# Hybrid decoder block: second buffers for the block rows and columns, masks and products with CB on VectorE, other waits for the delta heads

## The chip, the cores and the metric

The kernel runs on one core of one Trainium2 chip. The metric is the device time of one execution in microseconds (us), as the median of several runs.

## What is computed

One decoder layer for 256 tokens of width 2048 in float32: a SwiGLU (5632 wide) with half weight, a mixer of 8 delta heads (128 wide) and 16 state-space heads (64 wide) between one input and one output projection, a second SwiGLU, a gated per-layer embedding, and a final norm. Cut to what the change touches:

```python
def gated_delta_rule_chunked(q, k, v, g, beta):
    gc = jnp.cumsum(g, axis=-1)
    decay = jnp.exp(jnp.where(causal, gc[..., :, None] - gc[..., None, :], -jnp.inf))
    lower = jnp.where(strict, jnp.einsum('bnhik,bnhjk->bnhij', kb, k) * decay, 0.0)
    t_inv = lax.linalg.triangular_solve(eye + lower, eye, left_side=True, lower=True)
    ...
def ssd_chunked(x, dt, a_neg, bm, cm):
    seg = jnp.exp(jnp.where(causal, acs[..., :, None] - acs[..., None, :], -jnp.inf))
    cb = jnp.einsum('bnlgd,bnsgd->bngls', cc, bc)
    y_diag = jnp.einsum('bngrls,bnsgrp->bnlgrp', cb[:, :, :, None] * seg, xc)
    ...
h = h + 0.5 * swiglu(rmsnorm(h, ffn1_norm), ...)
proj = rmsnorm(h, mix_norm) @ w_in
o_gdn = gdn_mixer(...)   # delta heads
o_ssm = ssd_mixer(...)   # state-space heads
h = h + jnp.concatenate([o_gdn, o_ssm], axis=-1) @ w_out
```

## The kernel before

**Main work.** All activations lie transposed (features on the partitions). Every large weight is loaded in float32 by SyncE's queue (L110), and each piece of 128x1024 is split into a rounded part `hi` by ScalarE (L118) and the remainder `lo` by VectorE (L119); TensorE then multiplies `hi` and `lo` with the split activations. In the mixer `single` (L135) does this: a tile of 128 columns of `w_in` is two pieces, a piece is 24 matmuls (three each for eight blocks, L145 to L147). `project` makes two tiles, `conv_silu` lets the short convolution (L557) and SiLU follow, `silu_gate` the gate.

**Side work.** After every piece `tick` (L174) steps each generator in the list `side` once, up to its next `yield`. The generators are the scalars of the heads (`scalars`), the decay matrices (`early_decays`, `late_decay`), a pair of delta heads (`gdn_pair`, four times) and four state-space heads (`ssd_quad`, four times). A `yield` thus says how many pieces of main work are emitted between two steps. The order in which the instructions of an engine stand in its queue is made at build time by a planner (`schedule_with_timeline_sim=True`): emission gives the rank, and the planner's own model of times decides what is ready. Each engine then works its queue off in order.

**Decay.** A row of summed gates is spread over the partitions by DMA (`spread`, L447, tile `hT`, which is free in this stage). `decay` adds the causal mask to it, 128x512 at a time, on GpSimd (L453): one instruction for a pair, two for a quad, so 12 in all. ScalarE exponentiates (L457). `ssd_quad` multiplies the quad's decay with `CB` on GpSimd (L820), two instructions of 128x512 for each quad, 8 in all, before the matmuls of L832 read them.

**A pair of delta heads.** `kk` products (L596) and decay give `LA`. Its 32x32 blocks on the diagonal are written to DRAM by four DMAs of GpSimd's queue (L630, `blkl`) and come back with the block rows on the partitions (`Lb`, L632, SyncE's queue). VectorE then solves 31 columns one after the other (L663 and L665, `tb` and `Z`, 62 short instructions, `STEP = 3` columns for each tick), the result goes to DRAM (`blky`, L666) and back in four DMAs (`Y`, L671), and after `WAIT = 4` ticks VectorE transposes it (L674, `oT`). The blocks of 32 are put together to 64 and 128 by matmuls (`ip`, `ix`, `iy`, L685), then follow the products with the values (`two`, L714), the norm of the heads, four ticks, and the transposes back (`ot`, L758). `Lb` and `Z` have one buffer each (4 KB and 512 B of a partition), so a pair's block rows and columns wait for the pair before it; `qs` (1 KB) and `o` (2 KB) have one buffer of their own, `S` has one, `xv` two.

**Order of the mixer.** Pair 0, keys, pair 1, keys, pair 2, quad 0, pair 3, quads 1 to 3, then gates. Pair 3 has 40 ticks between its start and the point where the main work drains it, and its generator has 38 `yield`s once its decay is ready.

Of the kernel before, what the change touches and what calls it, by code (L numbers as in the profile page):

```python
# [9 lines left out]
F32 = mybir.dt.float32  # L10
F32R = mybir.dt.float32r
AF = mybir.ActivationFunctionType
ALU = mybir.AluOpType
PSUM = bass.MemoryType.PSUM

P = 128
# [27 lines left out]
BS = 32  # L44
CG = 4
# [4 lines left out]
WAIT = 4  # L50
STEP = 3
# [17 lines left out]
def tile_hybrid_block(ctx, tc, xT, pT, con, par, wgu1, wd1, wnar, win, wout, wgu2, wd2, wproj, wple, outT):  # L69
    nc = tc.nc  # L70
    act, dve, pool, pe = nc.scalar, nc.vector, nc.gpsimd, nc.tensor
# [17 lines left out]
    ident, upper, cmask = (cont[:, i * P:(i + 1) * P] for i in range(3))  # L89
# [3 lines left out]
    def pv(name):  # L93
        o, c = POFF[name]
        return part[:, o:o + c]

    def over(ap, n):
        return ap.unsqueeze(1).to_broadcast([ap.shape[0], n, ap.shape[-1]])
# [5 lines left out]
    def mx_bank(name):  # L104
        return psx.tile([P, 512], F32, tag="mx", name=name)
# [256 lines left out]
    with ExitStack() as mix:  # L362
# [76 lines left out]
        def quad_dec(i):  # L439
            k = (8, 12, 0, 4)[i]  # L440
            return hT[:, k:k + 4, :].rearrange("p k (n i) -> p (k n) i", i=P).rearrange("p (c n) i -> p c n i", c=2)
# [7 lines left out]
        def decay(d, h0, n):  # L449

            flat = d.rearrange("p c n i -> p (c n) i")
            for m in range(0, 2 * n, 4):
                pool.tensor_tensor(out=flat[:, m:m + 4], in0=flat[:, m:m + 4], in1=over(cmask, 4), op=ALU.add)  # L453
            yield
            yield
            for m in range(2 * n):
                act.activation(flat[:, m, :], flat[:, m, :], AF.Exp,  # L457
                               bias=ngc[:, m // n, h0 + m % n:h0 + m % n + 1])
                if m % 2:
                    yield  # L460

        def quad_decay(i):


            d = quad_dec(i)
            ers[i] = m2.tile([P, 2, P], F32, tag="er", name="er")
            for hh in range(2):
                s = slice(64 * hh, 64 * hh + 64)
                act.activation(ers[i][s], d[s, 1].rearrange("p (j h) l -> p h j l", h=2)[:, hh], AF.Exp)
            yield from decay(d, 8 + 4 * i, 4)  # L470
            ready.add(("quad", i))
# [3 lines left out]
        def early_decays():  # L475
            for i in range(4):
                spread(pair_dec(i), rows[:, 2 * i:2 * i + 2, :])
                if i:
                    yield
            for i in range(2):  # L480
                yield from decay(pair_dec(i), 2 * i, 2)
                ready.add(("pair", i))
            for i in range(2):
                spread(quad_dec(i), rows[:, 8 + 4 * i:12 + 4 * i, :])
                yield
            for i in range(2, 4):
                yield from decay(pair_dec(i), 2 * i, 2)
                ready.add(("pair", i))
            for i in range(2):
                yield from quad_decay(i)  # L490
# [85 lines left out]
        def gdn_pair(i, KQ, V):  # L576
# [16 lines left out]
            for c in range(2):  # L593
# [5 lines left out]
                for hh in range(2):  # L599
                    m = 2 * c + hh  # L600
# [6 lines left out]
                              in1=beta[:, :, h0:h0 + 2], op=ALU.mult)  # L607
            for m, (c, hh) in enumerate(mats):
                dve.scalar_tensor_tensor(
                    out=LA[:, m, :, :], in0=kk[c][:, hh * T:(hh + 1) * T].rearrange("p (a i) -> p a i", a=2),  # L610
# [17 lines left out]
            parts = [slice(q * BS, (q + 1) * BS) for q in range(P // BS)]  # L628
            for q, p in enumerate(parts):
                nc.gpsimd.dma_start(bl.rearrange("(m b) j i -> b j m i", m=4)[q], LT[p, :, p])  # L630
            Lb = g2.tile([P, BS, BS], F32, tag="Lb", name="Lb", bufs=1)
            nc.sync.dma_start(Lb.rearrange("p j i -> p (j i)"),  # L632
                              bl.rearrange("q j i -> q (j i)").unsqueeze(1).to_broadcast([P // NG, NG, BS * BS]))
            Z = g2.tile([P, CG, BS], F32, tag="Z", name="Z", bufs=1)
            tb = g2.tile([P, CG * BS], F32, tag="tb", name="tb", bufs=1)

            Y = g2.tile([P, 4, P], F32, tag="Y", name="Y")
# [6 lines left out]
            xv = g2.tile([P, 4, P], F32, tag="xv", name="xv")  # L644
# [9 lines left out]
            for _ in range(4):  # L654
                yield
            dve.tensor_copy(Z, unit)

            for j in range(BS - 1):
                if j % STEP == 0:
                    yield  # L660
                n = BS - 1 - j
                t = tb[:, :CG * n].rearrange("p (c n) -> p c n", n=n)
                dve.tensor_tensor(out=t, in0=over(Lb[:, j, j + 1:], CG),  # L663
                                   in1=Z[:, :, j:j + 1].to_broadcast([P, CG, n]), op=ALU.mult)
                dve.tensor_tensor(out=Z[:, :, j + 1:], in0=Z[:, :, j + 1:], in1=t, op=ALU.subtract)  # L665
            nc.gpsimd.dma_start(by.rearrange("q c i -> (q c i)").rearrange("(p f) -> p f", p=P),  # L666
                              Z.rearrange("p c i -> p (c i)"))

            X = oT[:, h0:h0 + 2, :].rearrange("p n (m i) -> p (n m) i", i=P)
            for q, p in enumerate(parts):  # L670
                nc.gpsimd.dma_start(Y[p, :, p], by.rearrange("(m b) c i -> b c m i", m=4)[q])  # L671
            for _ in range(WAIT):
                yield
            dve.transpose(X, Y)  # L674

# [16 lines left out]
            S = g2.tile([P, 2, P], F32, tag="S", name="S", bufs=1)  # L692
# [21 lines left out]
                    pe.matmul(ps[:, hh * P:(hh + 1) * P], lhs[hh], rhs[:, hh, :], start=True, stop=True)  # L714
                return ps[:, 0:T].rearrange("p (h v) -> p h v", h=2)

            qs = g2.tile([P, 2, P], F32, tag="qs", name="qs", bufs=1)
            o = g2.tile([P, 4, P], F32, tag="o", name="o", bufs=1)
            y0, y1 = xv[:, 0:2, :], xv[:, 2:4, :]
            ps = two([Y[:, hh, :] for hh in range(2)], y0, "y0")  # L720
            act.copy(y0, ps)
# [9 lines left out]
            for hh in range(2):  # L731
                dve.scalar_tensor_tensor(out=y1[:, hh, :], in0=pk[:, hh, :], scalar=negc[:, h0 + hh:h0 + hh + 1],
                                         in1=y1[:, hh, :], op0=ALU.mult, op1=ALU.add)
# [17 lines left out]
            pool.tensor_tensor(out=ro, in0=ro, in1=rq, op=ALU.mult)  # L751
            for m in range(4):
                act.mul(o[:, m, :], o[:, m, :], ro[:, m:m + 1])
            for _ in range(4):
                yield
            ps = mx_bank("ot")
            for m, (c, hh) in enumerate(mats):
# [4 lines left out]
        g2 = gdn_pool.enter_context(tc.tile_pool(name="g2", bufs=2))  # L762
# [20 lines left out]
        CB = mp.tile([P, 4, P], F32, name="CB")  # L783
# [15 lines left out]
        def ssd_quad(i, XS):  # L799

            g = i // 2
            h0 = 4 * i
            while ("quad", i) not in ready:
                yield
            d, er = quad_dec(i), ers[i]
            ds = [d[:, c] for c in range(2)]
            yield
            ps = mx_bank("xt")
            for c in range(2):
                for j in range(2):  # L810
                    pe.transpose(ps[:, (2 * c + j) * P:(2 * c + j + 1) * P], XS[:, j, c * P:(c + 1) * P], ident)
            xd = m2.tile([P, 2, 4, 64], F32, tag="xd", name="xd", bufs=1)
            for c in range(2):
                dve.tensor_tensor(out=xd[:, c], in0=ps[:, c * T:(c + 1) * T].rearrange("p (h v) -> p h v", h=4),
                                  in1=dt[:, c, h0:h0 + 4].unsqueeze(2).to_broadcast([P, 4, 64]), op=ALU.mult)
            xe = m2.tile([P, 4, 64], F32, tag="xe", name="xe", bufs=1)
            dve.tensor_tensor(out=xe, in0=xd[:, 0],
                              in1=dte[:, 8 + h0:12 + h0].unsqueeze(2).to_broadcast([P, 4, 64]), op=ALU.mult)
            for c in range(2):
                pool.tensor_tensor(out=ds[c], in0=ds[c], in1=over(CB[:, 2 * c + g, :], 4), op=ALU.mult)  # L820
            yield
            yield
            ps = mx_bank("ss0")
            pe.matmul(ps[:, 0:T], Bt[:, g, :], xe.rearrange("p h v -> p (h v)"), start=True, stop=True)
            St = m2.tile([P, 2, P], F32, tag="St", name="St", bufs=1)
            act.copy(St, ps[:, 0:T].rearrange("p (j v) -> p j v", j=2))
            yield
            py = mx_bank("py")
            for j in range(2):
                for hh in range(2):  # L830
                    for c in range(2):
                        pe.matmul(py[hh * 64:(hh + 1) * 64, j * T + c * P:j * T + (c + 1) * P],  # L832
                                  xd[:, c, 2 * j + hh, :], ds[c][:, 2 * j + hh, :], start=True, stop=True)
            ps = mx_bank("yo")
            for j in range(2):
                pe.matmul(ps[:, j * P:(j + 1) * P], St[:, j, :], BC[:, 1, g, P:T], start=True, stop=True)
            dve.tensor_tensor(out=er, in0=ps[:, 0:T].rearrange("p (j l) -> p j l", j=2), in1=er, op=ALU.mult)
            for j in range(2):
                t = 2 * i + j
                dve.scalar_tensor_tensor(out=yT[:, t, :], in0=XS[:, j, :], scalar=pv("sd")[:, t:t + 1],  # L840
                                         in1=py[:, j * T:(j + 1) * T], op0=ALU.mult, op1=ALU.add)
            dve.tensor_tensor(out=yT[:, 2 * i:2 * i + 2, P:T], in0=yT[:, 2 * i:2 * i + 2, P:T], in1=er, op=ALU.add)
# [53 lines left out]
        op = mix.enter_context(tc.tile_pool(name="op", bufs=1))  # L896
# [183 lines left out]
```

## Time and profile before

| | |
|---|---|
| median of 3 runs | 2077.48 us (2076.0 to 2078.01) |
| the profiled execution | 2078.17 us |
| its span, first to last instruction | 2076.3 us |
| TensorE busy | 2050.2 us, 99% of the span |
| VectorE, ScalarE, GpSimd busy | 1364.6, 1036.3, 174.5 us |
| mean granted clock of TensorE | 0.995 |

Times in the rows are microseconds from the first instruction, durations are microseconds unless marked ns. PE is TensorE, DVE VectorE, ACT ScalarE, POOL GpSimd, SP SyncE; SPq is the queue of DMAs that SyncE issues. Line numbers are those of the kernel before. The mixer lies between about 770 and 1207 us.

### The profile page before, as it was taken

How to read it: one execution, taken by the hardware profiler on the slowest of the kernel's cores; microseconds unless marked ns; L12 is line 12 of the kernel's file. 1: busy time of each engine (PE TensorE's matmuls, PEld its weight loads, DVE VectorE, ACT ScalarE, POOL GpSimd, SP SyncE). 2: the span in 40 equal slices, each digit the busy share in tenths (PEclk: the TensorE clock that was granted, in tenths of full speed). 3: DMA queues.
4: the chain of work that ended last, by engine and by line, in shares of the span. 5: the costliest groups of instructions: out<-in, count | busy, mean ns of one | idle time of the engine just before them, and what ended most of it. 6: DMA issues, size and time to landing. Idle time of an engine off the chain costs nothing.

```text
span 2076.3 us, 31518 instructions
## 1 busy us (share of the span) xinstructions
PE 2050.2 (99%) x12882; PEld 1833.7 (88%) x12882; DVE 1364.6 (66%) x2060; ACT 1036.3 (50%) x1542; POOL 174.5 (8%) x207
## 2 busy tenths in 40 slices
PE   9999999999999999999999999999999999999997
PEld 7888888888888889989999998888888888888886
DVE  7565555555656669999887666556555565556675
ACT  6444444444444556645545456444444444445554
POOL 2000000000000013313321111000000000000011
PEclk9999999999999999999999999999999999999998
DMA  7555555655555666544544555555556555545652
GB/s 263 191 185 183 173 175 192 210 183 185 189 182 178 198 223 213 180 165 163 176 166 168 186 182 186 196 185 183 168 182 217 184 183 185 190 162 189 207 183 102
DMA packets 64369, 384.58 MB, mean 185 GB/s; under 512 B 7616, under 2 KB 9168, under 8 KB 31072
## 3 DMA queue, kind: packets, MB, share of 16 engines
q1 hardware_dynamic: 61456, 376.75, 52.6%
q0 software_dynamic: 2480, 5.29, 0.8%
q8 instruction: 101, 1.65, 0.3%
q10 hardware_dynamic: 288, 0.52, 0.1%
q14 instruction: 44, 0.36, 0.0%
HBM read 377.78 MB, written 4.75 MB: 184 GB/s over the span
## 4 chain that ended last, share of the span: by engine, by line
PE 91%; DVE 3%; DMA 2%; issue 2%; POOL 1%; ACT 1%; POOLq 0%; DVEq 0%; SPq 0%; ACTq 0%
PE mm L130 50%; PE mm L128 24%; PE mm L146 4%; PE mm L147 4%; PE mm L145 4%; PE mm L132 1%; DMA hT<-rows 1%; DVE lo L119 1%; DVE u L557 1%; PE pj L130 0%; PE ip L685 0%; DMA blky<-Z 0%; DMA blkl<-LA 0%; PE iy L685 0%; POOL hT L820 0%
## 5 line engine op out<-in xcount | busy, mean ns | idle before, releaser
L119 DVE TENSOR_TENSOR lo<-raw,hi 128x1024 fp32r<-128x1024 f32 (+1 forms) x774 | 859.0, 1117 | 481.2 <-ACT hi L118 480.6
L130 PE MATMUL mm<-xs,hi 128*128 128x512 f32 x3088 | 1078.4, 397 | 1.1 <-DVE xs L190 1.0
L118 ACT CAST hi<-raw 128x1024 fp32r<-128x1024 f32 (+1 forms) x774 | 745.3, 964 | 566.0 <-PE mm L130 368.9
L128 PE MATMUL mm<-xs,lo 128*128 128x256 f32 x2895 | 812.7, 281 | 2.0 <-DVE lo L119 2.0
L130 PEld LDWEIGHTS mm<-xs,hi 128*128 128x128 f32 x3088 | 568.0, 188 | 124.9 <-DVE xs L190 1.6
L128 PEld LDWEIGHTS mm<-xs,lo 128*128 128x128 f32 x2895 | 543.5, 188 | 13.3 <-DVE lo L119 3.3
L130 PE MATMUL mm<-hid,hi 128*128 128x512 f32 x1408 | 492.5, 397 | 0.0
L128 PE MATMUL mm<-hid,lo 128*128 128x256 f32 x1344 | 377.8, 281 | 0.0
L130 PEld LDWEIGHTS mm<-hid,hi 128*128 128x128 f32 x1408 | 260.2, 188 | 59.0
L128 PEld LDWEIGHTS mm<-hid,lo 128*128 128x128 f32 x1344 | 253.3, 188 | 3.0
L147 PE MATMUL mm<-xs,lo 128*128 128x256 f32 x816 | 230.1, 282 | 3.5 <-DVE lo L119 3.5
L145 PE MATMUL mm<-xs,hi 128*128 128x256 f32 x816 | 230.4, 282 | 0.0
L146 PE MATMUL mm<-xs,hi 128*128 128x256 f32 x816 | 229.7, 281 | 0.0
L147 PEld LDWEIGHTS mm<-xs,lo 128*128 128x128 f32 x816 | 155.1, 190 | 4.0 <-DVE lo L119 3.9
L146 PEld LDWEIGHTS mm<-xs,hi 128*128 128x128 f32 x816 | 155.2, 190 | 0.4
L145 PEld LDWEIGHTS mm<-xs,hi 128*128 128x128 f32 x816 | 154.8, 190 | 0.6 <-issue 0.3
L168 ACT COPY t<-mm 128x256 f32<-128x256 f32 x167 | 62.4, 374 | 161.3 <-PE mm L130 160.4
L205 POOL TENSOR_TENSOR acc<-acc,sq 128x512 f32<-128x512 f32 x43 | 62.4, 1452 | 945.6 <-ACT sq L204 921.2
L169 DVE TENSOR_TENSOR t<-t,mm 128x256 f32<-128x256 f32 x167 | 70.0, 419 | 87.6 <-ACT t L168 87.3
L168 ACT COPY s<-mm 128x256 f32<-128x256 f32 x88 | 32.8, 373 | 148.9 <-PE mm L130 148.8
L169 DVE TENSOR_TENSOR s<-s,mm 128x256 f32<-128x256 f32 x88 | 37.1, 421 | 73.9 <-ACT s L168 73.8
L147 PE MATMUL mm<-osp,lo 128*128 128x256 f32 x256 | 71.8, 281 | 0.0
(299 smaller groups left out, 1450.7 us busy)
## 6 DMA issues: line engine op xcount, KB each, us to landing
raw<-in_wgu SPq DMA_DIRECT2D x173, 1024.0 KB, 4.8
raw<-in_wd SPq DMA_DIRECT2D x128, 704.0 KB, 4.1
raw<-in_win SPq DMA_DIRECT2D x52, 1024.0 KB, 4.8
raw<-in_wout SPq DMA_DIRECT2D x16, 1024.0 KB, 4.8
raw<-in_wple SPq DMA_DIRECT2D x16, 1024.0 KB, 4.8
first<-in_wgu SPq DMA_DIRECT2D x11, 256.0 KB, 7.6
hold<-hT POOLq DMA_DIRECT2D x4, 512.0 KB, 3.8
Lb<-blkl SPq DMA_DIRECT2D x4, 512.0 KB, 4.6
```

What stands on the lines that cost most here:

```text
L118: act.copy(hi, src)
L119: dve.tensor_tensor(out=lo, in0=src, in1=hi.bitcast(F32), op=ALU.subtract)
L128: pe.matmul(ps[:, 0, :], lo[:, w, :], act_in[:, k, 0, :], start=False, stop=False, skip_group_check=True)
L130: pe.matmul(ps, hi[:, w, :], act_in[:, k], start=start, stop=stop, skip_group_check=True)
L132: pe.matmul(ps[:, 0, :], lo[:, w, :], act_in[:, k, 0, :], start=False, stop=False, skip_group_check=True)
L145: pe.matmul(ps[:, 0, :], hi[:, i, :], act_in[:, k, 0, :], start=k == ks[0], stop=False)
L146: pe.matmul(ps[:, 0, :], hi[:, i, :], act_in[:, k, 1, :], start=False, stop=False)
L147: pe.matmul(ps[:, 0, :], lo[:, i, :], act_in[:, k, 0, :], start=False, stop=k == ks[-1])
L168: act.copy(out, ps[:, 0, :])
L169: dve.tensor_tensor(out=out, in0=out, in1=ps[:, 1, :], op=ALU.add)
L205: pool.tensor_tensor(out=acc, in0=acc, in1=sq, op=ALU.add)
L557: dve.scalar_tensor_tensor(out=u[:, j, :], in0=cin[:, j, k:k + T], scalar=cw[:, j, k:k + 1], in1=u[:, j, :], op0=ALU.mult, op1=ALU.add)
```

## The change

The mask adds of `decay` and the products with `CB` move from GpSimd to VectorE, and one of two ticks between mask and exponential goes. `Lb` and `Z` get two buffers (the pool's default); `qs` lies in `S` and `o` in `xv`. Pairs 0 to 2 wait three ticks more for the columns from DRAM (7), pair 3 as before (4). Pair 3 solves four columns for each tick, so that its 31 columns take 8 ticks in place of 11, and waits three ticks in place of four before the transposes.

```diff
@@ decay
             for m in range(0, 2 * n, 4):
-                pool.tensor_tensor(out=flat[:, m:m + 4], in0=flat[:, m:m + 4], in1=over(cmask, 4), op=ALU.add)
-            yield
+                dve.tensor_tensor(out=flat[:, m:m + 4], in0=flat[:, m:m + 4], in1=over(cmask, 4), op=ALU.add)
             yield
@@ gdn_pair
-            Lb = g2.tile([P, BS, BS], F32, tag="Lb", name="Lb", bufs=1)
+            Lb = g2.tile([P, BS, BS], F32, tag="Lb", name="Lb")
...
-            Z = g2.tile([P, CG, BS], F32, tag="Z", name="Z", bufs=1)
+            Z = g2.tile([P, CG, BS], F32, tag="Z", name="Z")
...
-                if j % STEP == 0:
+                if j % (STEP if i < 3 else STEP + 1) == 0:
                     yield
...
-            for _ in range(WAIT):
+            for _ in range(WAIT if i == 3 else WAIT + 3):
                 yield
             dve.transpose(X, Y)
...
-            qs = g2.tile([P, 2, P], F32, tag="qs", name="qs", bufs=1)
-            o = g2.tile([P, 4, P], F32, tag="o", name="o", bufs=1)
+
+            qs, o = S, xv
...
-            for _ in range(4):
+            for _ in range(4 if i < 3 else 3):
                 yield
@@ ssd_quad
             for c in range(2):
-                pool.tensor_tensor(out=ds[c], in0=ds[c], in1=over(CB[:, 2 * c + g, :], 4), op=ALU.mult)
+                dve.tensor_tensor(out=ds[c], in0=ds[c], in1=over(CB[:, 2 * c + g, :], 4), op=ALU.mult)
```

## Rows read from the trace of the kernel before

**Rows 1.** The page, part 1: busy time, share of the span, instructions.
```profile
PE 2050.2 (99%) x12882; PEld 1833.7 (88%) x12882; DVE 1364.6 (66%) x2060; ACT 1036.3 (50%) x1542; POOL 174.5 (8%) x207
```
**Rows 2.** Windows: stretch, length, busy (count) by engine, clock, DMA share, GB/s.
```profile
820.00:1010.00 190.00, 182.84 (x1556) 180.94 (x1555) 178.34 (x450) 104.34 (x194) 59.44 (x81) 0.98 0.50 172
1010.00:1050.00 40.00, 37.93 (x340) 36.56 (x338) 32.15 (x77) 20.62 (x38) 13.95 (x22) 1.00 0.53 180
1050.00:1120.00 70.00, 70.00 (x615) 69.07 (x614) 50.21 (x105) 35.45 (x69) 16.03 (x25) 1.00 0.46 161
```
**Rows 3.** PE's waits, 770 to 1120: waiter, releaser, total, times, longest.
```profile
PE ip L685 <- DVE oT L674: 5.0, 2, 3.7
PE mm L147 <- DVE lo L119: 3.5, 2, 2.2
PE y L714 <- DVE Y L690: 0.6, 1, 0.6
```
**Rows 4.** Windows with the lower granted clock.
```profile
835.00:840.00 5.00, 4.58 (x26) 4.58 (x27) 4.96 (x9) 4.50 (x12) 2.00 (x3) 0.66 0.46 120
...
910.00:915.00 5.00, 2.25 (x15) 2.25 (x16) 4.84 (x11) 2.49 (x3) 0.00 (x0) 0.89 0.49 179
915.00:920.00 5.00, 5.00 (x36) 5.00 (x36) 5.00 (x13) 2.29 (x3) 0.00 (x0) 0.77 0.50 167
```
**Rows 5.** Timeline (start, length, instruction, [idle before]): DVE, then POOL, around 830.
```profile
826.42 7.48 DVE L557 SCALAR_TENSOR_TENSOR u<-cin,gcw,u 128x256 f32<-128x256 f32 x3 [1.20 <-ACT u L552]
...
852.75 0.88 DVE L557 SCALAR_TENSOR_TENSOR u<-cin,gcw,u 128x256 f32<-128x256 f32 x2
...
827.90 3.79 POOL L453 TENSOR_TENSOR hT<-hT,cont 128x512 f32<-128x512 f32 x3
...
831.82 1.28 POOL L453 TENSOR_TENSOR hT<-hT,cont 128x512 f32<-128x512 f32 x1
```
**Rows 6.** Timeline around 880: DVE, then POOL.
```profile
878.98 2.96 DVE L557 SCALAR_TENSOR_TENSOR u<-cin,gcw,u 128x256 f32<-128x256 f32 x2
...
884.55 1.28 DVE L663 TENSOR_TENSOR tb<-Lb,Z 128x40 f32<-128x40 f32 x1
...
877.97 7.81 POOL L820 TENSOR_TENSOR hT<-hT,CB 128x512 f32<-128x512 f32 x5 [4.88 <-DVE CB L793]
```
**Rows 7.** Groups by line and shape: count, busy us, mean ns, idle before.
```profile
L453 POOL TENSOR_TENSOR hT<-hT,cont 128x512 f32<-128x512 f32 x12 | 18.0, 1514 | 30.7 <-ACT er L469 24.5 <-DMA hT<-rows 6.2
...
L344 DVE TENSOR_TENSOR t<-t,rh 128x512 f32<-128x512 f32 x32 | 22.0, 687 | 0.0
```
**Rows 8.** POOL's waits, 775 to 1120.
```profile
POOL hT L453 <- DMA hT<-rows: 6.2, 4, 2.4
```
**Rows 9.** Timeline: pair 0's columns to DRAM, back, and their transposes.
```profile
899.89 0.61 POOL L666 DMA_DIRECT2D blky<-Z  x1 [14.11 <-DVE Z L665]
907.09 2.19 POOL L671 DMA_DIRECT2D Y<-blky  x4 [6.59 <-DMA blky<-Z]
...
911.99 0.71 DVE L674 STREAM_TRANSPOSE oT<-Y 128x512 f32<-128x512 f32 x1 [0.16 <-DMA Y<-blky]
```
**Rows 10.** Timeline: pair 1's block rows asked for; pair 3 waiting for Z and Lb.
```profile
898.41 0.54 SPq L632 DMA_DIRECT2D Lb<-blkl  x1
...
1015.95 0.23 DVE L656 COPY Z<-cont 128x128 f32<-128x128 f32 x1 [2.96 <-DMA blky<-Z]
...
1020.47 0.29 DVE L663 TENSOR_TENSOR tb<-Lb,Z 128x124 f32<-128x124 f32 x1 [3.16 <-DMA Lb<-blkl]
```
**Rows 11.** Windows of the instructions on tile tb alone: stretch, length, DVE busy.
```profile
907.00:955.00 48.00, 13.24 (x59) 0.96 0.43 149
```
**Rows 12.** Timeline: pair 2's xv written; pair 0's and pair 3's heads transposed back.
```profile
946.94 1.15 ACT L646 ACTIVATE xv<-vt,irk 128x128 f32<-128x128 f32 x4 [1.48 <-PE o L714]
...
976.95 0.61 PE L758 MATMUL ot<-cont,o 128*128 128x128 f32 x4
...
1115.84 0.27 PE L758 MATMUL ot<-cont,o 128*128 128x128 f32 x1
```

## The prediction, made before the change was run

> **What bounds the kernel now.** First the page's busy times: PE is busy for 2050.2 of 2076.3 us [rows 1], so only its 26 idle us and the stretches at a lower clock can be won, whatever the other engines save. Next the windows of the mixer, the only stage that the change touches: PE lacks 190 - 182.8 = 7.2 us between 820 and 1010 and 2.1 us between 1010 and 1050, and nothing between 1050 and 1120 [rows 2]. The rest of the 26 us lies at the start and the end of the program. Third, who ended these waits [rows 3]: `lo` of the main work (3.5 us in two waits, the longest 2.2), the transposed columns `oT` (5.0 us in two, the longest 3.7), and 0.6 us for `Y`. In order of time I call them A (2.2 us, before 835, `lo`), B (1.3 us, before 887, `lo`), C (3.7 us, before 913, `oT` of pair 0), D (1.3 us, before 1024, `oT` of pair 2) and E (0.6 us, before 1046).
>
> Fourth, the clock. Behind A and behind C the granted clock falls to its lower level, 1.2 in place of 2.4 GHz, for a few us: 0.66 over 5 us, and 0.89 and 0.77 over 5 us each [rows 4]. The loss in full-speed time is 0.34 x 5 = 1.7 us behind A and (0.11 + 0.23) x 5 = 1.7 us behind C. Behind B and D the windows stay at 1.00 [rows 2]. All that the change can win is then 7.2 + 2.1 + 3.4 = **12.7 us**: a floor of 2077.5 - 12.7 = 2064.8 us.
>
> Fifth, VectorE is busy for 178.3 of 190 us from 820 to 1010 [rows 2], so it is a second limit there, and what it loses comes out in A, B and C.
>
> **Part 1: masks and products leave GpSimd.** Beside four mask adds on POOL (3.79 and 1.28 us), three of DVE's convolution steps took 7.48 us, where two of them take 0.88 elsewhere, so three take 1.3: 6.2 us lost [rows 5]. `lo`, queued behind, came late, and that is A. Beside the products with `CB` on POOL, five DVE instructions ran from 878.98 to 885.83, 6.9 us, in place of some 1.8 (three convolution steps at 0.44, two short ones of the solve at about 0.25): 5.1 us lost [rows 6]. That is B. So 11.3 us of VectorE's time are lost in these two places; the remaining moved instructions overlap with DVE less.
>
> The Trainium skill, page "SBUF — State Buffer", section "Who interferes with whom", states that a DVE instruction with two SBUF inputs and a GpSimd instruction that reads SBUF exclude each other: the one that starts second is blocked until the first is done. The trace agrees (7.48 us above). By that rule the moved instructions, which have two SBUF inputs too, could still be held by what stays on POOL. By the rows the gain is the 11.3 us; by the rule it would be at most the 18.0 us of mask adds and somewhat less for the products, and the time predicted would be the same, since PE's waits cap it.
>
> What comes in its place: 12 + 8 = 20 instructions of 128x512 on DVE at 0.69 us (0.687 for L344, against 1.51 on POOL [rows 7]): 13.8 us, of which the eight early masks, 5.5 us, fall before 907 and the other twelve, 8.3 us, later, spread over more than 100 us. In the critical stretch DVE therefore gains 11.3 - 5.5 = 5.8 us, more than A's 2.2 and B's 1.3 us. I take both waits as gone, with A's clock loss: **-5.2 us**.
>
> The move adds a wait: a mask add waits for its row's DMA, and POOL stood 6.2 us in four such waits, the longest 2.4 [rows 8]. On DVE the convolution and `lo` are queued behind it, and PE behind `lo`. POOL's queue loses the 20 instructions, so the DMA issues behind them (L630, L666, L671) can only come earlier. Price of the new wait: between 0 (`lo` is made ahead; a DVE wait of 2.96 us at 1016 stood in no PE wait [rows 3, 10]) and 2.4 + 1.7 = 4.1 us (the same fall of the clock as behind A). I take 1.3, because the near row of 2.96 us cost nothing and one such wait of B's size is likely somewhere. The tick taken out between mask and exponential lets the decay come one piece earlier; no PE wait hangs on it, so 0.
>
> **Part 2: two buffers for Lb and Z.** Pair 1's `Lb` was asked for at 898.41, when pair 0's solve was nearly done, and pair 3's solve stood 2.96 us for `Z` and 3.16 us for `Lb` [rows 10]. With two buffers the solves of neighbours overlap. That moves up to a solve's 13.2 us of DVE time [rows 11] forward, pair 1's by some 25 us. It gives PE nothing by itself. `S` for `qs` and `xv` for `o` add no instruction, but they hold buffers longer: see the third rival.
>
> **Part 3: three more ticks for the columns.** From the issue of `blky` to the end of the transposes pair 0 took 911.99 + 0.71 - 899.89 = 12.8 us [rows 9]. A tick is 24 matmuls, and 615 of them took 70 us [rows 2], so a tick is 2.7 us: four ticks are 10.9 us, less than the way through DRAM, and seven are 19.1. So C and D should go. What speaks against: the planner places `ip` where its own model has `oT` ready, and in the code `ip` of pair 0 is emitted long before the place that it has on PE, so the ticks may not bind at all. But most of C was made by part 1's loss: pair 0's solve stood still on DVE for the time of rows 6, about 5 us against 1.3 of PE, so without it `oT` comes some 3.8 us earlier against PE, which is C's 3.7. I take C with its clock loss as gone, **-5.4 us**. D comes from POOL's queue (an issue behind four others); I take half of it, **-0.7**. E stays: the sum of squares that held VectorE there is still on POOL.
>
> **Part 4: pair 3.** Of its 38 yields the solve loses 3 and the end 1, so 34 are left for the 40 ticks. Its last transposes ended at 1116 [rows 12] with no PE wait behind them up to 1120 [rows 2], so this is worth 0; it is cover against a pair 3 that comes later.
>
> **Sum.** -5.2 - 5.4 - 0.7 + 1.3 = -10.0 us. The profiled execution took 2078.2 us (span 2076.3 and 1.9 around it), 0.7 above the median of the runs. 2078.2 - 10.0 - 0.7 = **2067.5 us**.
>
> **Rivals.** (1) The planner's model decides, and C stays. For it: `ip` stands where a model that knows too short a way through DRAM has put it. Against it: C has the size of part 1's loss. Gain A and B alone, 5.2 us: 2072.3, with 2070.5 to 2075 as its own range.
>
> (2) VectorE becomes the bound: slower. Place: 820 to 907. Masks (5.5 us) and half of pair 1's solve brought forward (6.6 us) ask for 12.1 us more, against 11.3 us that the locks give back, if they do. If instructions with the same inputs are held by what is left on POOL, `lo` is late by 12.1 us less some 4 us of DVE's idle time there; A, B and C stay, and a clock loss of 1.7 us or so stands behind one wait in two of them: 2077.5 + 8 = 2085.5. It decides from the point where the locks give back less than the 12.1 us less the idle time, 8 us. For it: 178 of 190 us busy. Against it: the lock time stands in the rows, and a wait that A shows took POOL's 128x512 work.
>
> (3) New waits take the place of the old: the change does nothing that can be seen. Pair 2's `xv` was written at 946.94, as soon as pair 0's product with it was done; now the buffer is free only after pair 0's transposes back, 976.95, 30 us later [rows 12]. ScalarE stands in order, with `hi` behind that write. If the planner is wrong there by as much as it was at C (3.7 + 1.7 = 5.4 us), for pairs 2 and 3: 2067.5 + 10.8 = 2078.3.
>
> **How the numbers follow.** Chances: forecast 0.57 (own range 2064.0 to 2070.5), rival 1 0.23, rival 3 0.12, rival 2 0.08. From the floor 2064.8, less 0.8 for the scatter of runs, to 2077.0: that takes in the forecast, rival 1 and a part of rival 3, and leaves out about 0.17. A measurement of this kernel tells some 0.2%, 4.2 us, from no change. Faster than 2073.3: 0.57 + 0.18 of rival 1 = 0.75. Within 2073.3 to 2081.6: 0.05 + 0.12 = 0.17. Slower: 0.08.
>
> **What would show it.** Part 1: no convolution step of several us around 830 and 880, masks at 0.7 us on DVE, no PE wait on `lo`; wrong, if PE waits on `lo` where a mask stands on DVE. Part 2: pair 1's `Lb` is asked for right after its blocks have landed. Part 3: no PE wait on `oT`, clock at 1.00 from 820 to 1050. The prediction is wrong if PE's idle time from 770 to 1120 is above 5 us, or if an ACT wait for `ot` stands ahead of a late `hi`.

## The result, and the profile after

| | before | after |
|---|---|---|
| median of the runs (6 each, same chip) | 2077.47 us | 2088.7 us (2087.52 to 2090.42) |
| ratio, 95% interval | | 1.0054 (1.0045 to 1.0064) |
| span of the profiled execution | 2076.3 us | 2086.8 us |
| TensorE without work, 770 to 1240 us | 9.2 us | 12.5 us |
| last matmul of the mixer's main work starts | 1121.5 us | 1117.5 us |
| first matmul of the output projection starts | 1121.6 us | 1128.5 us |

The changed kernel is 0.54% slower, where 0.5% faster was forecast. Line numbers below L453 are those of the changed kernel, one less than before behind `decay`; an experiment's are its own kernel's.

First the page and the windows of the mixer, columns as in [rows 1] and [rows 2]:

```profile
PE 2057.4 (99%) x12882; PEld 1837.9 (88%) x12882; DVE 1362.3 (65%) x2080; ACT 1035.1 (50%) x1542; POOL 140.8 (7%) x187
...
820.00:1010.00 190.00, 185.72 (x1575) 182.81 (x1574) 170.14 (x435) 104.27 (x186) 36.72 (x66) 1.00 0.53 177
1010.00:1050.00 40.00, 38.57 (x340) 37.69 (x338) 35.22 (x83) 23.70 (x48) 9.96 (x18) 1.00 0.59 195
1050.00:1120.00 70.00, 69.08 (x599) 66.85 (x598) 52.96 (x123) 29.49 (x52) 9.05 (x17) 1.00 0.44 153
```

Against [rows 2], TensorE did more up to 1010 (1575 matmuls, 1556 before). VectorE carries 20 instructions more in all, and yet its busy time between 820 and 1010 fell from 178.3 to 170.1 us. It does not work more; it stands. Who ended its waits between 815 and 1085, and those of TensorE between 770 and 1130 (total, times, longest):

```profile
DVE hT L453 <- DMA hT<-rows: 9.4, 6, 3.2
DVE lo L119 <- ACT hi L118: 5.8, 12, 1.9
DVE tb L662 <- DMA Lb<-blkl: 5.1, 2, 3.4
...
PE ot L757 <- ACT xv L752: 6.0, 3, 3.7
PE mm L147 <- DVE lo L119: 3.2, 1, 3.2
PE mm L145 <- ACT osp L195: 1.2, 1, 1.2
PE o L713 <- ACT xv L736: 0.9, 1, 0.9
PE snrow L249 <- DVE sn L214: 0.9, 1, 0.9
```

The 6.2 us for which GpSimd stood for the rows [rows 8] are 9.4 us of VectorE now. On TensorE, B to E are gone, the `oT` waits altogether, and in A's place, 4 us later, stands another wait for `lo`. Of what came instead two things matter (two waits for `ot`, at 976 and 1022, make 2.3 us).

The first, at 836, is 3.2 us for `lo`. VectorE's timeline there (start, length, instruction, idle before and its releaser):

```profile
828.09 0.69 DVE L453 TENSOR_TENSOR hT<-hT,cont 128x512 f32<-128x512 f32 x1 [2.25 <-DMA hT<-rows]
...
829.84 1.29 DVE L453 TENSOR_TENSOR hT<-hT,cont 128x512 f32<-128x512 f32 x2
...
837.21 0.29 DVE L662 TENSOR_TENSOR tb<-Lb,Z 128x124 f32<-128x124 f32 x1 [3.43 <-DMA Lb<-blkl]
...
838.39 1.22 DVE L119 TENSOR_TENSOR lo<-raw,hi 128x1024 fp32r<-128x1024 f32 x1
```

A mask waits 2.25 us for its row, then the first step of pair 0's solve waits 3.43 us for its block rows, and the `lo` that TensorE needs stands behind both.

The second is the end of the mixer. TensorE's timeline from its last main matmul, then the windows with the lower granted clock:

```profile
1117.50 0.28 PE L147 MATMUL mm<-xs,lo 128*128 128x256 f32 x1
...
1119.58 0.71 PE L713 MATMUL o<-xv,LA 128*128 128x128 f32 x4 [0.92 <-ACT xv L736]
1121.20 1.02 PE L249 MATMUL snrow<-cont,sn 128*128 128x128 f32 x4 [0.90 <-DVE sn L214]
1125.91 1.36 PE L757 MATMUL ot<-cont,xv 128*128 128x128 f32 x4 [3.70 <-ACT xv L752]
1128.51 0.77 PE L145 MATMUL mm<-osp,hi 128*128 128x256 f32 x2 [1.24 <-ACT osp L195]
```
```profile
1120.00:1125.00 5.00, 1.31 (x7) 0.83 (x5) 2.80 (x9) 1.28 (x8) 2.04 (x7) 0.64 0.58 211
1125.00:1130.00 5.00, 2.79 (x9) 1.90 (x10) 2.07 (x4) 3.98 (x10) 0.35 (x2) 0.50 0.00 0
1130.00:1135.00 5.00, 5.00 (x25) 5.00 (x25) 3.50 (x6) 2.04 (x4) 0.64 (x1) 0.50 0.00 0
```

The main work is done at 1117.5, 4.0 us earlier than before, but pair 3 is not: its heads are transposed back at 1125.9, where before that was over at 1116 [rows 12]. For 11.0 us TensorE has only the remains of pair 3, and its clock is at the lower level (0.50) until 1135, into the output projection. Sum against the span: -4.0 for the main work, +10.9 for the end without main work (11.0 against 0.1), +3.3 for the output projection, which took 94.3 us in place of 91.0: +10.2 of the +10.5 us.

What is late is pair 2's and then pair 3's solve. Of each the first and last instruction on `tb` and `Z`, worked out from the trace:

| solve | before | after |
|---|---|---|
| pair 0 | 839.5 to 899.6 | 837.2 to 917.4 |
| pair 1 | 907.4 to 955.9 | 917.4 to 955.8 |
| pair 2 | 963.7 to 1007.9 | 960.4 to **1038.8** |
| pair 3 | 1020.5 to 1062.6 | 1038.9 to 1080.8 |

In pair 2's solve the profile of after has this on VectorE; before, the solve was through at that time, 1007.9:

```profile
1010.01 0.22 DVE L664 TENSOR_TENSOR Z<-Z,tb 128x56 f32<-128x56 f32 x1
1013.46 0.69 DVE L453 TENSOR_TENSOR hT<-hT,cont 128x512 f32<-128x512 f32 x1 [3.23 <-DMA hT<-rows]
1014.07 0.20 DVE L662 TENSOR_TENSOR tb<-Lb,Z 128x52 f32<-128x52 f32 x1
```

### The profile page after: what moved, and what is told of

It is laid out like the page before. It is cut to its first block, busy times and chain, and to the rows that moved or that the text cites. A ratio compares the mean times of both kernels' runs of the same rounds, so it can differ in the third digit from the quotient of the medians.

```text
span 2086.8 us, 31528 instructions
## 1 busy us (share of the span) xinstructions
PE 2057.4 (99%) x12882; PEld 1837.9 (88%) x12882; DVE 1362.3 (65%) x2080; ACT 1035.1 (50%) x1542; POOL 140.8 (7%) x187
## 5 line engine op out<-in xcount | busy, mean ns | idle before, releaser
L128 PEld LDWEIGHTS mm<-xs,lo 128*128 128x128 f32 x2895 | 543.5, 188 | 13.3 <-DVE lo L119 3.2
L145 PE MATMUL mm<-osp,hi 128*128 128x256 f32 x256 | 73.2, 287 | 1.2 <-ACT osp L195 1.2
```

What stands on the lines that cost most here:

```text
L128: pe.matmul(ps[:, 0, :], lo[:, w, :], act_in[:, k, 0, :], start=False, stop=False, skip_group_check=True)
L145: pe.matmul(ps[:, 0, :], hi[:, i, :], act_in[:, k, 0, :], start=k == ks[0], stop=False)
```

## The experiments

All are medians with the kernel before on the same chip beside them. The first four were to tell three theories apart. **Theory 1**: the move and the ticks together make the end without main work. **Theory 2**: the move alone does it, through VectorE. **Theory 3**: the ticks alone do it.

**e1, the changed kernel with four ticks.**
```diff
-            for _ in range(WAIT if i == 3 else WAIT + 3):
+            for _ in range(WAIT):
```


> The changed kernel with four ticks (as before) for the columns of pairs 0 to 2; all else of the change stays. Theory 1 (the mixer runs out of main work: in the changed kernel the last piece of the mixer's main work is done at 1117.3 us and the first matmul of the output projection starts at 1128.5, since pair 3 ends too late, and that comes from the moved instructions and the three more ticks together): the 10.9 us without main work and the 3.3 us at the lower clock behind them go, 2088.7 - 14.2 = 2074.5, between 2071 and 2079. Theory 2 (VectorE's load: 20 more instructions and their waits for DMAs in its queue make the loss, whatever the ticks): 2085 to 2089. Theory 3 (the three ticks alone make pair 3 late): as before or better, 2071 to 2079.

2084.72 us, 1.0034 (1.0023 to 1.0046). The end without main work is gone (0.1 us), but TensorE stands 8.7 us at `ip` of pair 2. With the masks on VectorE, the ticks only choose where the late pair is paid for.

**e2, the move alone** (masks and products on VectorE, one tick less, nothing else of the change).

> The kernel before with the masks and the products with CB on VectorE, and one tick less between mask and exponential; buffers and ticks as before. Theory 1: no time without main work at the end of the mixer, the waits on lo of before replaced by others of their size, 2073 to 2080. Theory 2: most of the loss is here, 2084 to 2089. Theory 3: 2073 to 2080.

2090.04 us, 1.006 (1.0039 to 1.0082). TensorE's waits, and the windows around the long one:

```profile
PE ip L684 <- DVE oT L673: 12.6, 1, 12.6
PE mm L147 <- DVE lo L119: 3.3, 2, 3.0
...
1030.00:1035.00 5.00, 0.00 (x0) 0.00 (x0) 1.58 (x6) 0.00 (x0) 1.56 (x3) 0.50 0.89 292
1035.00:1040.00 5.00, 1.10 (x4) 1.01 (x5) 4.22 (x16) 0.00 (x0) 0.62 (x2) 0.50 0.13 42
1040.00:1045.00 5.00, 5.00 (x31) 4.46 (x29) 4.23 (x17) 0.37 (x1) 0.00 (x0) 0.50 0.08 15
```
The whole loss is in the move, with the tick that goes with it, so Theories 1 and 3 fall. Pair 2's solve ends at 1028.5.

**e3, the ticks alone**, and **e4, all but the move** (buffers and ticks; masks and products on GpSimd).

> The kernel before with the change's ticks alone: seven ticks for the columns of pairs 0 to 2, four columns for each tick and three ticks at the end for pair 3. Theory 1: pair 3 still ends in time, 2073 to 2079. Theory 2: 2075 to 2079, since VectorE's load is that of before. Theory 3: the loss is here, 2085 to 2090.

> The changed kernel with masks and products back on GpSimd (and both ticks behind the mask): buffers and ticks alone. Theory 1: pair 3 ends earlier than before, no time without main work, 2072 to 2078. Theory 2: 2074 to 2078. Theory 3: 2085 to 2090.

e3: 2077.72 us, 1.0 (0.999 to 1.001). e4: 2077.27 us, 0.9996 (0.9986 to 1.0005). Neither does anything alone, in e4 against my forecast of part 3.

The move has two halves, which e5 and e6 part. From here on **Theory W** says that the masks cost by standing for their rows in VectorE's queue, and **Theory B** that they cost by VectorE's busy time.

**e5, the products alone; e6, the masks alone** (with one tick less).
```diff
e5:  pool.tensor_tensor(out=ds[c], ...)  ->  dve.tensor_tensor(out=ds[c], ...)
e6:  pool.tensor_tensor(out=flat[:, m:m + 4], ...)  ->  dve.tensor_tensor(...), and one yield less
```


> The kernel before with the eight products with CB on VectorE and nothing else. The move alone cost 12 us. Theory W (the masks stand in VectorE's queue waiting for the DMA of their rows, 9.5 us in all with the move alone, and everything behind them comes late; products wait for no DMA): 2074 to 2080. Theory B (VectorE's own busy time: the solves get only what the main work leaves, and 20 instructions of 0.69 us put pair 2's solve off): eight of twenty, 2080 to 2084.

> The kernel before with the twelve masks on VectorE and one tick less behind them; products stay on GpSimd. Theory W: the whole loss, 2086 to 2092. Theory B: twelve of twenty, 2082 to 2087.

e5: 2075.8 us, 0.999 (0.9981 to 1.0). B is gone, and so is C; 2.3 us are won, at the edge of the noise. e6: 2087.46 us, 1.0049 (1.0035 to 1.0064). The loss is in the masks, or in the tick that left with them: no run here has the masks on VectorE and both ticks. Waits of e6 (from an execution of 2091.1 us):

```profile
PE ip L684 <- DVE oT L673: 10.9, 2, 7.9
PE mm L147 <- DVE lo L119: 3.0, 1, 3.0
...
DVE hT L453 <- DMA hT<-rows: 8.5, 4, 3.6
```

**e7, the wait alone.** The masks stay on GpSimd; ahead of each, VectorE copies one column of the same row.
```diff
+                dve.tensor_copy(touch, flat[:, m, 0:1])
                 pool.tensor_tensor(out=flat[:, m:m + 4], in0=flat[:, m:m + 4], in1=over(cmask, 4), op=ALU.add)
```


> The kernel before, masks on GpSimd, but ahead of each mask VectorE copies one column of the same rows (128x1): it waits for the same DMA and is busy for nearly nothing. Theory W: 2083 to 2090. Theory B: 2076 to 2080.

2085.79 us, 1.0037 (1.0024 to 1.005). The group of these copies (count, busy us, mean ns, idle before):

```profile
L454 DVE COPY touch<-hT 128x1 f32<-128x1 f32 x12 | 1.8, 151 | 8.3 <-DMA hT<-rows 8.2
```
Twelve copies with 1.8 us of work and 8.2 us of waiting make the kernel 7.7 us slower, with both ticks in place. Waiting is enough, almost without work. TensorE's waits:

```profile
PE ip L687 <- DVE oT L676: 4.4, 2, 2.9
PE cb L793 <- DVE BC L563: 2.9, 1, 2.9
PE mm L147 <- DVE lo L119: 2.9, 2, 2.6
```
The masks on GpSimd wait for the copies in their turn (7.4 us in five waits, where before they waited 6.2 us for the rows), which a mask on VectorE does not bring.

**e8, the busy time alone, and e13, the same held in place.** A dummy of 128x512 on constants on VectorE ahead of each mask, which stays on GpSimd; in e13 with a scalar that ScalarE makes from the convolution's input of that moment. In both, `qs` lies in `S` and `o` in `xv`, to make room.
```diff
e8:  +  dve.tensor_tensor(out=spare, in0=lmask4, in1=over(cmask, 4), op=ALU.add)
e13: +  act.mul(late, cin[:, 0, 3:4], 0.0)
     +  dve.scalar_tensor_tensor(out=spare, in0=lmask4, scalar=late, in1=over(cmask, 4), ...)
```


> The kernel before, masks on GpSimd, but ahead of each mask VectorE adds two constant tiles of 128x512 into a spare one: the masks' busy time without their wait for the DMA (qs and o lie in S and xv, to make room for the spare tile). Theory W: 2076 to 2081. Theory B: 2082 to 2087.

> The kernel before, masks still on GpSimd, plus on VectorE ahead of each of the 12 masks one 128x512 instruction on constants, with a scalar that ScalarE makes from the convolution's input of that moment, so that it cannot be moved far forward (and qs in S, o in xv, for room). It gives VectorE the busy time of the masks, some 12 x 0.7 = 8.3 us, without their wait for the rows. Theory W (the wait in the queue costs): 2076 to 2080. Theory B (the busy time costs, since VectorE has no time to spare): 2083 to 2088, with the solves of pairs 0 and 2 stretched as in the changed kernel.

e8: 2089.18 us, 1.0056 (1.0041 to 1.0072). It tells nothing: the dummies wait for nothing, so all of them stand between 762 and 780, ahead of the heads' scalars, and the rows go to DRAM at 816.7 in place of 808.75. e13: 2095.59 us, 1.0085 (1.007 to 1.01):

```profile
L457 DVE SCALAR_TENSOR_TENSOR spare<-cont,late 128x512 f32<-128x512 f32 x12 | 9.0, 746 | 0.0
```
9.0 us of work without a wait cost 17.4 us. Two dummies still stand ahead of the scalars (796.6 and 806.7) and the rows go out 2.7 us late (811.46), so the size is not all busy time in the stretch. TensorE's longest waits:

```profile
PE ot L763 <- ACT xv L758: 6.8, 1, 6.8
PE ip L690 <- DVE oT L679: 4.7, 1, 4.7
PE mm L145 <- DVE cin L384: 3.3, 1, 3.3
```
Ahead of the longest, at 1037, ScalarE had stood 4.2 us for `ro`, the norm of the heads from GpSimd, a way that neither theory names. So this run doesn't price the busy time, but it speaks against W's claim that only the wait costs.

**e9, the masks back.** The changed kernel, masks on GpSimd again (still one tick less).

> The changed kernel with one edit undone: the masks go back to GpSimd; products, buffers and ticks stay as changed. If the masks on VectorE are the cause of the loss in the changed kernel too: 2073 to 2079, at or below the kernel before. If products, buffers and ticks cost something together that none costs alone: 2082 to 2088.

2075.86 us, 0.9995 (0.9986 to 1.0004): of the 11.2 us that the changed kernel loses against before, nothing is left (-0.7).

**e10 and e12, the masks held until their rows have landed.** In e10 the masks alone, in e12 the changed kernel. The quads' eight masks take a zero that ScalarE makes from the convolution's input at that point, so that they stand later in the queue.
```diff
+                late = m2.tile([P, 1], F32, tag="late", name="late")
+                act.mul(late, cin[:, 0, 3:4], 0.0)
...
+                    dve.scalar_tensor_tensor(out=flat[:, m:m + 4], in0=flat[:, m:m + 4], scalar=late, in1=over(cmask, 4),
+                                             op0=ALU.add, op1=ALU.add)
```


> The kernel with the masks alone on VectorE, but each mask of a quad also takes a column of zeros that ScalarE makes from the convolution's input of the tick at which the mask is emitted. So it can't be put into VectorE's queue ahead of that tick, its row has landed by then, and its busy time of 0.69 us stays. Theory W (the waits for the DMA): about 7.8 of 9.5 us of waits go, 2076 to 2081. Theory B (the busy time): 2084 to 2089, as with the masks alone.

> The changed kernel with the quads' masks gated as in the run of gated masks. Theory W: the waits for the rows leave VectorE's queue, 2077 to 2083. Theory B: 2085 to 2090.

e10: 2080.05 us, 1.0014 (1.0005 to 1.0023), so 3.5 us are lost in place of 9.3 in e6, with nearly the same work on VectorE (8.5 us in place of 8.2). e12: 2078.63 us, 1.0008 (0.9999 to 1.0018): 2.1 us lost in place of 11.2. Waits for rows in e10, two lines for the two kinds of mask; in e12 they are 1.7 and 1.1 us:

```profile
DVE hT L457 <- DMA hT<-rows: 3.2, 1, 3.2
DVE hT L460 <- DMA hT<-rows: 1.6, 3, 1.0
```
The hold also moves busy time: four masks that stand between 824 and 830 in e6 stand between 845 and 858 in e10, so these two runs do not part the wait from the place of the work. The end without main work stays in e12 (11.0 us).

**e14, e12's kernel with four ticks.**

> The changed kernel with the quads' masks held back until their rows have landed (as in the run before it), and with 4 ticks in place of 7 for the columns of pairs 0 to 2. If the three ticks make the dry end of the mixer (too little is left for pair 3), the first output-projection matmul follows the last piece at once and the time is 2070 to 2075. If the ticks are needed against the wait for the transposed columns, that wait comes back (4 to 8 us) and the time is 2079 to 2084. If neither, 2077 to 2080.

2082.27 us, 1.0028 (1.0019 to 1.0038). The end without main work goes, a wait of 12.1 us at `ip` of pair 2 takes its place. So with the masks on VectorE pair 2 is late even when they hardly wait (its solve ends at 1020.6 and 1022.1 in e12 and e14, at 1007.9 before). A part of that may be the tick that both lack: with the masks on GpSimd and that tick gone (e9) the solve ends at 1016.7.

**e11, the best of the parts, and e15, the same with four ticks.** Products on VectorE, two buffers, the shorter way of pair 3, in e11 seven ticks; the masks on GpSimd with both ticks behind them, as before.

> All that did no harm alone: products on VectorE, two buffers, the change's ticks; masks on GpSimd with both ticks behind them. If the gains of the products (2 us) and of buffers and ticks (nothing to 1 us) add up: 2073 to 2076. If they don't: 2076 to 2079.

> Products with CB on VectorE, two buffers, shorter solve of pair 3, masks on GpSimd as before, but 4 ticks in place of 7 for pairs 0 to 2. If the ticks carry the gain of the best version (they take away C and D, some 6 us), the time is 2073 to 2077. If products and buffers do it by an earlier solve, 2068 to 2071 as with the ticks.

e11: **2069.35 us**, 0.9963 (0.9951 to 0.9976), below both kernels. e15: 2079.09 us, 1.001 (1.0001 to 1.002), with 6.6 us at `ip` of pair 2. Windows and waits of e11:

```profile
820.00:1010.00 190.00, 188.17 (x1615) 185.75 (x1615) 181.26 (x465) 108.22 (x202) 56.47 (x80) 1.00 0.54 184
1010.00:1050.00 40.00, 39.75 (x345) 38.05 (x345) 37.78 (x99) 18.96 (x36) 7.78 (x16) 1.00 0.48 165
1050.00:1120.00 70.00, 70.00 (x615) 69.81 (x614) 50.62 (x88) 37.97 (x69) 12.87 (x25) 1.00 0.45 160
...
PE mm L147 <- DVE lo L119: 1.8, 1, 1.8
PE ip L685 <- DVE Z L665: 0.2, 1, 0.2
```
TensorE lacks 2.1 us, at A, and the clock stays at its upper level. The output projection begins at 1113.7 in place of 1121.6.

## Why the prediction was wrong

**What bounds the kernel** held in the main: what can be won or lost is TensorE's idle time and the clock behind it. In e11, where both nearly vanish, the kernel takes 2069.35 us, 7.2 less than before on the same chip; the floor was 2064.8. The two do not account for everything: in e7 the profiled span is 5.1 us longer than before, with 3.4 us more idle time but 6.3 us less at the lower clock; where the rest lies these runs do not show.

**Part 1 failed, in the step "The move adds a wait".** It was priced from 0 to 4.1 us and taken at 1.3, because a VectorE wait of 2.96 us before [rows 10] stood in no wait of TensorE. That row was the wrong one to lean on: it is one wait, and the masks bring four to six of them, 8.5 to 9.5 us in e2, e6 and the changed kernel. And the step looked for the wait's victim only in `lo`. The other thing queued behind it is the serial solve, which gets what VectorE has left over from the main work. VectorE was busy for 178 of 190 us; 12 us were all that it had to spare.

A second step of part 1 failed on its own rows, the sum for the critical stretch: "the eight early masks, 5.5 us, fall before 907 and the other twelve, 8.3 us, later". The five products at 878 [rows 6] fall before 907 too, and a ninth mask:

```profile
871.65 1.29 POOL L453 TENSOR_TENSOR hT<-hT,cont 128x512 f32<-128x512 f32 x1 [2.37 <-DMA hT<-rows]
```
That makes 14 of the 20 instructions, 14 x 0.69 = 9.6 us: the gain there was 11.3 - 9.6 = 1.7 us and not 5.8, less than A and B (3.5 us), before any new wait; and five of the changed kernel's six waits for rows, 6.1 us, fall there as well.

So the account of VectorE's time has to hold three terms: the work that is added, the time that instructions no longer stretch beside GpSimd's, and the waits that come along. From the traces (one execution each): all the work that was added, and of 815 to 1030 us the rest; stretched time is what instructions took beyond 1.25 times the median of their line and shape (15.1 us before):

| kernel | work added | stretched time saved | waits for rows | sum | median against before |
|---|---|---|---|---|---|
| e5 products | 5.1 | 5.8 | 0 | -0.7 | -2.3 |
| e6 masks | 8.2 | 8.7 | 8.5 | +8.0 | +9.3 |
| e7 wait alone | 1.8 | 1.0 | 8.2 | +9.0 | +7.7 |
| e10 masks held | 8.5 | 9.8 | 4.9 | +3.6 | +3.5 |
| e2 move | 13.3 | 15.1 | 9.5 | +7.7 | +12.4 |
| after | 13.3 | 15.1 | 9.4 | +7.6 | +11.2 |
| e12 after, held | 13.8 | 15.1 | 2.8 | +1.5 | +2.1 |
| e14 the same, four ticks | 13.8 | 15.1 | 3.0 | +1.7 | +4.1 |
| e13 dummies | 9.0 | 6.0 | 0 | +3.0 | +17.4 |

(e5, e2: the durations of the changed kernel's groups, 8.2 us for 12 masks and 5.1 for 8 products.) In these rows but the last the sign comes out, and in most of them the size; work and saving nearly cancel in the changed kernel, and what is left is the wait. But the account knows nothing of ticks and buffers, and for kernels that change them with the masks on GpSimd, without a wait for rows, it fails: e11 has 5.1 us of work and 3.1 saved, +2.0, where -7.2 was measured; e15 5.2 and 8.2, -3.0, where +0.9 was measured; e3 alone has 3.2 us more stretched time and lost nothing. So its fit is support and no proof. That the masks on VectorE make the changed kernel's loss is shown (e9), and that waits like theirs are enough for a loss of that size (e7); that the wait, and not the masks' busy time, is the main part is the likeliest reading of e7, e10 and e12, but argued. The last row doesn't fit, and some 2 to 5 us of e2, e14 and after are left over. Whether VectorE's time costs more than its length there, or the other order of instructions that each edit brings about, these runs do not settle.

The other half of part 1 was right. The stretched steps at 826 and 878 [rows 5, 6] are gone; the five products take 3.09 us on VectorE where GpSimd took 7.81, and B goes with them alone in e5. How much of that time reaches TensorE is another matter: e11, the fastest kernel, still has 12.0 of the 15.1 us. The Trainium skill, page "SBUF — State Buffer", section "Who interferes with whom", has the lock as the reason, and the traces agree: 15.1 us of stretched time before, none in the changed kernel, and with the masks back on GpSimd (e11) three convolution steps take 7.25 us again. The Trainium skill, page "GPSIMD Engine Reference", section "4.1 Engine selection", sends an elementwise operation on a tile to VectorE; by length the trace agrees (0.69 us against 1.51), by time of the kernel it does so for the products and not for the masks, which wait for a DMA (e5 against e6).

"The tick taken out ... so 0" failed too, beside masks on GpSimd: e9 and e11 differ in that tick alone, 2075.86 against 2069.35 us, and pair 2's solve ends at 1016.7 in e9, at 1007.7 in e11. So a part of the changed kernel's late pair 2 may be the tick's; with the masks on VectorE this is untested.

**Part 2** said that the solves of neighbours overlap. They don't: in the changed kernel and in e11 each begins when the one before it has ended, or later (904.3 and 904.8 in e11). The second buffer did what was forecast of it, and it was not enough: pair 1's block rows are asked for at 873.98 in place of 898.41 and have landed by 879, but the solve begins at 917.4.

```profile
873.98 0.54 SPq L631 DMA_DIRECT2D Lb<-blkl  x1
```
What goes is the gap between some of them, such as 7.8 us between pairs 0 and 1 before (899.6 to 907.4).

**Part 3** was right that C and D go, but not for one reason, and wrong in its independence. D, the wait at `ip` of pair 2, goes with the ticks: in all eleven kernels here with four ticks it stands, 1.3 to 12.6 us, and in the six with seven there is none above 0.3 us. C goes with the products, whatever the ticks: none of the nine kernels with the products on VectorE has it (e1, e2, e5, e14 and e15 have four ticks), and six of the eight with the products on GpSimd have it (1.8 to 3.7 us; e10 has 0.4, e13 none). That fits the prediction's remark that most of C was made by part 1's loss, but not its reason, an `oT` that comes earlier: in e5 pair 0's solve ends at 905.6 in place of 899.6, and C is gone because `ip` stands later still on TensorE, at 920.8 in place of 912.8. Why it stands there is not shown. Ticks alone give 0 (e3), ticks and buffers 0.4 us (e4), products and buffers without the three ticks a loss of 0.9 us (e15), all three a gain of 7.2 us (e11). I had added up terms that hold only together.

**Part 4 failed too**: it put the end of pair 3 at 0, as cover, and gave no price for a pair 3 that uses the cover up. That price was what mattered: +14.2 us (10.9 without main work, 3.3 in the output projection behind it, which starts at the lower clock), against 4.0 won before it. The heads of pair 3 were transposed by 1116 and the output projection began at 1121.6; after, pair 3's solve ends 18 us later (1080.8 against 1062.6). A margin of 5 us was no cover against that.

**The rivals.** Rival 2 had the sign and nearly the size (2085.5; chance 0.08), and its premise, VectorE without time to spare, was right. With 9.6 us for the moved work in place of 5.5 it asks for 16.2 us, and its own condition (the locks give back less than that less 4 us of idle time: 11.3 against 12.2) was met on paper before the run. What it feared did not come, locks that stay: they did give their time back, and busy time fell; the waits came in their place. Rival 3 looked for the new wait in `xv` and ScalarE; where ScalarE waited at `xv` in the changed kernel, most of it (9.9 us in three waits) was for `ro`, the norm of the heads from GpSimd, not for the buffer, and e4, with `qs` and `o` in the same buffers, loses nothing. Rival 1's doubt, that the order built ahead of time decides where `ip` stands, fits e1, e2, e14 and e15, where `ip` of pair 2 stands 6.6 to 12.6 us too early on TensorE. That the order's model takes the DMAs of rows and blocks to land sooner than they do (the rows' DMAs have medians of 6.4 and 12.1 us from issue to landing) is argued, not shown.

The range left out a loss. The profile had the warning: a wait row of 6.2 us on GpSimd, busy for 59 of 190 us, to be moved to an engine with 12 us to spare [rows 2, 8].

## What to carry to other kernels

Before an instruction moves to another engine, read what it *waits* for: a wait that is free on an idle engine stops everything queued behind it on a full one, serial side work above all. Split a move by its inputs: here what found its inputs ready (the products) gained a little, and what stood for a DMA (the masks) lost, although the new engine did it in half the time. Count, from the rows, every moved instruction that falls into the stretch that decides. And a change that shifts when side work ends is priced at the last place that waits for it, here the end of the mixer, not only at the waits seen before.

## What the runs showed of the hardware

TensorE pays for a long wait twice. The granted clock falls to its lower level, 1.2 in place of 2.4 GHz, around the end of most waits above 2 us: for 3.4 us at a wait of 2.2 us (A, before) and at 3.0 us (e1, at 836); for 10.2 us at 6.6 us (e15) and 8.7 us (e1); for 13.7 us at 12.1 us (e14); for 17.1 us at 12.6 us (e2), each of these four in part within the wait itself. The wait's length does not settle it: 13.7 us stand at a wait of 3.9 us (e8, at 1035), and 20.5 us, the longest, at one of 7.9 us (e6, 1030.7 to 1051.2), where only the short matmuls of the side work follow up to 1047.5:

```profile
1045.00:1050.00 5.00, 5.00 (x26) 5.00 (x25) 4.13 (x9) 1.66 (x5) 1.06 (x1) 0.50 0.00 0
```
Nor do short waits behave alike: 1.8 us at A brought 3.4 us at the lower level in e3 and e4 and none in e11, and the 3.2 us at 836 in the changed kernel brought none. The prediction's flat 1.7 us is the price of one such 3.4 us stretch, and of short waits alone.
